# Score matmuls of differential attention on 128 rows, with stacked keys and head-wise projections

## The chip, the cores and the metric

The kernel runs on one core of a Trainium2 chip. The metric is the time of one execution on the device in microseconds (us). The engines are named as in the profile: PE is TensorE (matrix multiplications), PEld its weight loads, DVE is VectorE, ACT is ScalarE, POOL is GpSimd, SP is SyncE, which here only issues transfers. Each engine works through its own instruction list in order, and the engines wait for each other by semaphores. PSUM is the memory that PE writes, SBUF the one that it reads.

## The reference

A decoder trunk of two layers on 512 tokens of width 1024. Each layer normalizes x, projects it with one wide matrix, and runs three kinds of attention on parts of the result: differential attention (8 heads), latent attention (MLA, 8 heads) and attention into 256 memory tokens (cross, 4 heads). Their outputs are projected, gated, added and projected once more, and a squared-ReLU MLP follows. The change touches differential attention alone:

```python
def diff_attention(q, k, v, q_gain, k_gain, lam_vecs, out_gain, cos, sin, layer_idx):
    q = q.reshape(B, S, DIFF_HEADS, 2, DIFF_HEAD_DIM)      # 8 heads, 2 maps, 64
    k = k.reshape(B, S, DIFF_HEADS, 2, DIFF_HEAD_DIM)
    v = v.reshape(B, S, DIFF_HEADS, DIFF_V_DIM)            # 128
    q = rotary(rmsnorm(q, q_gain), c, s_)
    k = rotary(rmsnorm(k, k_gain), c, s_)
    o = causal_block_attention(q, k, v, DIFF_HEAD_DIM ** -0.5)
    ...
    o = o[:, :, :, 0, :] - lam.astype(o.dtype) * o[:, :, :, 1, :]
    o = rmsnorm(o, out_gain) * (1.0 - lam_init)
```

Each head has two score maps, each over 64 dimensions; the two softmaxes are subtracted with a factor and multiplied by one v.

## The kernel before

**Precision.** Operands of most matmuls are split into two parts, hi (rounded to the float32r type) and lo (the rest). A product is three matmuls: hi·hi, hi·lo, lo·hi. `mm3` (L108 to L111) issues the three for all projections. `split_into` (L100) makes the parts: ScalarE copies hi (L101), VectorE subtracts lo (L102).

**Weights.** Weights come from memory in units of at most 128x1024 (`wraw`, three buffers, L905) and are split into `whi` and `wlo` (four buffers each) ahead of use, in the order in which the program consumes them.

**Order.** `layer` builds a list of entries. Attention units are merged with GEMM entries stage by stage: `phases` (L882) names the attention units of nine stages, `PLAN` (L25) the GEMM groups that are spread between them by `merge` (L45). Stages 1 and 2 hold MLA, 3 holds cross attention, 4 to 7 hold two differential heads each (4 units a head), 8 none. In `PLAN`, `gx`, `gc` and `gd` are gate projections and what follows from them, `mem` the projections of memory tokens, `xq` the queries of cross attention, `ym` the output projection of MLA, and `d0` to `d3` the projections for differential attention. The framework then orders the instructions of each engine by a simulated timeline, with the program order as priority, so that work moves from its place in the list where a buffer or an operand is not there yet.

**Projections of differential attention.** `dpair(p)` (L858) makes three chunks for heads 2p and 2p+1: q, k and v, 256 columns each (`diff_chunk`, L553). A chunk is two entries of 96 matmuls in all; it fills two `psacc` buffers (there are two), each with two of the four token tiles, and `done` evicts each of these half chunks. For q and k: ScalarE copies it (L564) and squares it (L566), VectorE sums (L568), GpSimd takes the power −1/2 (L132), VectorE rotates and scales (L583 to L587), PE transposes (L591) into a `pstp` bank (there are two), and for each of the two heads `split_into` writes hi and lo of 128 rows, map 0 in rows 0 to 63 and map 1 in rows 64 to 127. V is copied with a scale (L561). All these results are tiles of the pool `B`, 24 of 128x512.

**Scores.** A unit of `diff_att` (L732) is one head and one block of 128 queries, with N = 128 to 512 keys. `scores` (L597) issues for each of the three hi/lo products the matmul of both maps in turn, into two of the three `pss` banks:

```python
            if diff:
                for i, (a, b) in enumerate(((0, 0), (0, 1), (1, 0))):
                    for m in range(2):
                        T.matmul(sw[m][:, :max(N, 256)], lhsT=qk[m][0][a], rhs=qk[m][1][b], start=i == 0, stop=i == 2)
```

This is L610: operands are slices of 64 rows. Then VectorE adds the mask (L622) and takes maxima (L624), ScalarE takes the exponential (L627), VectorE combines the maps (L630 to L632), PE transposes (L638) and multiplies with v (L642). There are 8 heads, 4 blocks and 2 layers: 64 units.

Of the kernel before, what the change touches and what calls it, by code (L numbers as in the profile page):

```python
# [24 lines left out]
PLAN = ["gx:1 K0 gx:1 Q0 gx:1 K1 gx:1 Q1", "gx mem", "xq d0", "d1 ym", "gc:6", "d2 gc", "d3", "gd:5", "gd"]  # L25
# [34 lines left out]
def tile_trunk(ctx: ExitStack, tc: tile.TileContext, x_t, mem_t, mem_n, pos, ifr, gcol, grow, w_ck, w_cq, w_kvb, w_qb,  # L60
# [68 lines left out]
    A.dma_start(out=gr, in_=grow[:, 0:128].partition_broadcast(P))  # L129

# [148 lines left out]
    def layer(l):  # L279
# [3 lines left out]
        def build_rope():  # L283
            for qk in range(2):
                a = sm.tile([P, NT, 64], F32, tag=f"ra{qk}", name=nm("ra"), bufs=1)
                b = sm.tile([P, NT, 64], F32, tag=f"rb{qk}", name=nm("rb"), bufs=1)
                for half in range(2):
                    g = gr[:, l, qk * 64 + half * 32:qk * 64 + (half + 1) * 32].unsqueeze(1).broadcast_to([P, NT, 32])
                    G.tensor_tensor(out=a[:, :, half * 32:(half + 1) * 32], in0=cosd, in1=g, op=ALU.mult)
                    G.tensor_tensor(out=b[:, :, (1 - half) * 32:(2 - half) * 32], in0=(sind if half == 0 else nsind), in1=g, op=ALU.mult)  # L290
                s["rope", qk] = (a, b)
# [261 lines left out]
        def diff_chunk(p, c):  # L553
            def done(tp, q):
                if tp == 0:
                    s["d", p, c] = [tl("B") for _ in range(2)] if c == 2 else [(tl("B", F32R), tl("B", F32R)) for _ in range(2)]
                dst = s["d", p, c]
                if c == 2:
                    for ti in range(2):
                        t = 2 * tp + ti  # L560
                        A.activation(out=dst[tp][:, ti * 256:(ti + 1) * 256], in_=q[:, ti * 256:(ti + 1) * 256], func=AF.Copy, scale=s["r"][:, t:t + 1])  # L561
                    return
# [8 lines left out]
                bc = lambda a: a[:, 2 * tp:2 * tp + 2].unsqueeze(2).broadcast_to([P, 2, 4])  # L571
                if c == 0:
                    V.tensor_tensor(out=ev, in0=sv, in1=bc(s["ex64"]), op=ALU.add)
                else:
                    V.scalar_tensor_tensor(out=ev, in0=sv, scalar=1.0 / 64, in1=bc(s["epsx"]), op0=ALU.mult, op1=ALU.add)
# [282 lines left out]
        def dpair(p):  # L858
            return diff_chunk(p, 0) + diff_chunk(p, 1) + diff_chunk(p, 2)
# [149 lines left out]
```

## Time and profile before

| what | value |
|---|---|
| median of 3 runs | 2037.0 us (2036.42 to 2038.12) |
| the profiled execution's own time | 2039.67 us |
| its span in the profile | 2037.6 us |
| PE busy | 2005.1 us (98%) |
| DVE busy | 1162.2 us (57%) |
| ACT busy | 917.4 us (45%) |
| POOL busy | 146.0 us (7%) |
| mean granted clock of PE | 0.994 |

The span reaches from the first to the last instruction of the program; the execution's own time is a little longer. Busy time of an engine is the time in which at least one of its instructions ran. Matmuls overlap in their pipeline, so the pace of PE is read from the starts of neighbouring instructions in the timeline and not from the duration of one. In the groups a line ends with its count, its busy time and the mean duration of one in ns, then the idle time of the engine before them. In the timeline a row gives start and length in us; neighbouring instructions of one kind are merged, with their count at the end.

### The profile page before, as it was taken

The page shows a single profiled execution, that of the slowest core. Times are in us where ns is not written, and L with a number is a line of the kernel's source. Part 1 is how long each engine was busy: PE and PEld are TensorE (multiplying, and loading weights), DVE is VectorE, ACT ScalarE, POOL GpSimd, SP SyncE. Part 2 cuts the span into 40 slices and gives each one's busy share as a digit, 9 for nine tenths or more (in the row PEclk, how much of TensorE's full clock was granted, in tenths as well). Part 3 has the DMA queues.
Part 4 walks back from the last instruction along what each step waited for, and adds up shares of the span by engine and source line. Part 5 has one row for each costly group of instructions (what it writes and reads, how often), then busy time and mean ns, then how long its engine had stood idle before and what let it go on. Part 6 is the DMA issues. An engine that isn't in the chain of part 4 may idle for free.

```text
span 2037.6 us, 27922 instructions
## 1 busy us (share of the span) xinstructions
PE 2005.1 (98%) x11008; PEld 1715.9 (84%) x11008; DVE 1162.2 (57%) x2170; ACT 917.4 (45%) x1727; POOL 146.0 (7%) x121
## 2 busy tenths in 40 slices
PE   8999999999999999999999999999999999999999
PEld 7779997888878888888888899979897788888887
DVE  7755765777656543434447567757686454434442
ACT  6666654444433432323346666634445334323321
POOL 0300110111200000000002001101020000000000
PEclk9989999999999999999999999999999999999999
DMA  5233122222214333333332321222222333333332
GB/s 170 73 110 102 69 63 73 63 73 73 63 53 154 93 96 101 93 99 98 117 104 67 125 80 63 72 74 63 73 63 63 101 116 93 102 96 94 102 94 73
DMA packets 54675, 181.06 MB, mean 89 GB/s; under 512 B 6416, under 2 KB 7440, under 8 KB 54544
## 3 DMA queue, kind: packets, MB, share of 16 engines
q1 hardware_dynamic: 51840, 175.66, 27.8%
q10 hardware_dynamic: 2704, 3.62, 0.6%
q8 instruction: 87, 1.43, 0.3%
q14 instruction: 44, 0.36, 0.1%
HBM read 175.06 MB, written 4.19 MB: 88 GB/s over the span
## 4 chain that ended last, share of the span: by engine, by line
PE 95%; ACT 2%; DVE 1%; DMA 1%; issue 0%; POOL 0%; ACTq 0%; DVEq 0%; POOLq 0%
PE psacc L109 21%; PE psacc L111 20%; PE psacc L110 20%; PE pss L109 7%; PE pss L111 7%; PE pss L110 7%; PE pss L610 2%; PE pss L613 2%; PE pso L642 2%; PE pstp L654 1%; PE pstp L638 1%; PE pstp L591 1%; PE pso L110 1%; PE pso L111 1%; PE pso L109 1%; PE pstp L479 1%
## 5 line engine op out<-in xcount | busy, mean ns | idle before, releaser
L101 ACT ACTIVATE whi<-wraw 128x1024 fp32r<-128x1024 f32 (+3 forms) x320 | 334.5, 1046 | 751.7 <-PE psacc L110 398.5
L102 DVE TENSOR_TENSOR wlo<-wraw,whi 128x1024 fp32r<-128x1024 f32 (+3 forms) x320 | 385.9, 1206 | 97.7 <-ACT whi L101 95.4
L109 PE MATMUL psacc<-H,whi 128*128 128x512 f32 x816 | 321.6, 394 | 2.6 <-ACT B L561 2.2
L110 PE MATMUL psacc<-H,whi 128*128 128x512 f32 x816 | 320.2, 392 | 0.0
L111 PE MATMUL psacc<-H,wlo 128*128 128x512 f32 x816 | 320.1, 392 | 0.0
L109 PE MATMUL psacc<-whi,H 128*128 128x256 f32 (+1 forms) x928 | 271.6, 294 | 10.3 <-ACT whi L101 6.8
L110 PE MATMUL psacc<-wlo,H 128*128 128x256 f32 (+1 forms) x928 | 265.1, 286 | 0.0
L111 PE MATMUL psacc<-whi,H 128*128 128x256 f32 (+1 forms) x928 | 264.3, 287 | 0.2 <-DVE H L106 0.2
L109 PE MATMUL pss<-O,whi 128*128 128x512 f32 x640 | 249.8, 392 | 1.6 <-ACT O L105 1.6
L110 PE MATMUL pss<-O,whi 128*128 128x512 f32 x640 | 250.8, 392 | 0.0
L111 PE MATMUL pss<-O,wlo 128*128 128x512 f32 x640 | 250.5, 392 | 0.0
L109 PEld LDWEIGHTS psacc<-whi,H 128*128 128x128 f32 x928 | 177.6, 192 | 17.8 <-ACT whi L101 6.8
L109 PEld LDWEIGHTS psacc<-H,whi 128*128 128x128 f32 x816 | 153.2, 188 | 36.0 <-ACT B L561 2.6
L111 PEld LDWEIGHTS psacc<-H,wlo 128*128 128x128 f32 x816 | 153.2, 188 | 33.6 <-issue 2.0
L110 PEld LDWEIGHTS psacc<-H,whi 128*128 128x128 f32 x816 | 153.3, 188 | 31.4 <-issue 0.7
L110 PEld LDWEIGHTS psacc<-wlo,H 128*128 128x128 f32 x928 | 178.2, 192 | 1.8 <-issue 1.0
L111 PEld LDWEIGHTS psacc<-whi,H 128*128 128x128 f32 x928 | 177.3, 192 | 1.0 <-DVE H L106 0.4
L840 DVE TENSOR_TENSOR X<-psacc,X 128x512 f32<-128x512 f32 x64 | 44.3, 692 | 207.1 <-PE psacc L111 207.1
L627 ACT ACTIVATE P<-pss,nmx 128x128 f32<-128x128 f32 (+2 forms) x224 | 115.1, 521 | 73.6 <-DVE nmx L624 47.5
L109 PEld LDWEIGHTS pss<-O,whi 128*128 128x128 f32 x640 | 120.4, 188 | 27.3 <-ACT O L105 2.0
L110 PEld LDWEIGHTS pss<-O,whi 128*128 128x128 f32 x640 | 121.1, 189 | 25.5 <-DVE O L106 0.3
L111 PEld LDWEIGHTS pss<-O,wlo 128*128 128x128 f32 x640 | 121.0, 189 | 24.9
(231 smaller groups left out, 3220.6 us busy)
## 6 DMA issues: line engine op xcount, KB each, us to landing
wraw<-in_w_dram SPq DMA_DIRECT2D x128, 512.0 KB, 3.6
wraw<-in_w_g_dram SPq DMA_DIRECT2D x48, 512.0 KB, 3.6
wraw<-in_w_d_dram SPq DMA_DIRECT2D x48, 512.0 KB, 3.6
wraw<-in_w_mem_dram SPq DMA_DIRECT2D x16, 512.0 KB, 3.7
wraw<-in_w_od_dram SPq DMA_DIRECT2D x16, 512.0 KB, 3.6
wraw<-in_w_out_dram SPq DMA_DIRECT2D x16, 512.0 KB, 3.7
X<-in_x_t_dram SPq DMA_DIRECT2D x16, 256.0 KB, 5.4
wraw<-in_w_xq_dram SPq DMA_DIRECT2D x8, 512.0 KB, 4.3
```

The source lines that it names most:

```text
L101: A.activation(out=hi, in_=src, func=AF.Copy)
L102: V.tensor_tensor(out=lo, in0=src, in1=hi, op=ALU.subtract)
L109: T.matmul(o, lhsT=l[0], rhs=r[0], start=first, stop=False, **kw)
L110: T.matmul(o, lhsT=l[0], rhs=r[1], start=False, stop=False, **kw)
L111: T.matmul(o, lhsT=l[1], rhs=r[0], start=False, stop=last, **kw)
L479: T.transpose(tp_[:96, t * P:(t + 1) * P], in_=src[t][:, h * 96:(h + 1) * 96], identity=ident)
L591: T.transpose(tp_[:, h * 256 + t * P:h * 256 + (t + 1) * P], in_=y[:, t * 256 + h * P:t * 256 + (h + 1) * P], identity=ident)
L610: T.matmul(sw[m][:, :max(N, 256)], lhsT=qk[m][0][a], rhs=qk[m][1][b], start=i == 0, stop=i == 2)
L613: T.matmul(sv[m], lhsT=qk[m][0], rhs=qk[m][1], start=True, stop=True)
L627: A.activation(out=pt[:, m, :N], in_=sv[m], func=AF.Exp, bias=nmx[:, m:m + 1], accum_out=ssum[m])
L642: T.matmul(o, lhsT=w[:, j * P:(j + 1) * P], rhs=vs(j), start=j == 0, stop=j == nb - 1)
L840: V.tensor_tensor(out=xt, in0=q, in1=xt, op=ALU.add)
```

## The change

- The q and k columns of the input projection are ordered by head: a chunk of 256 columns now holds q and k of one head (`head_chunk`), v keeps a chunk for two heads (`v_chunk`). The number of chunks and matmuls of the projections stays.
- `PLAN` names these chunks (`h0` to `h7`, `v0` to `v3`) in place of `d0` to `d3`, at other places between the attention units.
- For each map the keys' hi and lo lie in one tile `kk` of 128 rows, hi in the rows of the map and lo in the others. The queries' hi lies in both halves of `qh`, their lo in the rows of the map in `ql`, whose other half is set to zero by GpSimd. Two matmuls of 128 rows per map, `qh` with `kk` and `ql` with `kk`, give the sum of the three products.
- The eviction after the transposes is, for each of the two maps, three ScalarE copies and two VectorE subtractions of 64 rows and 256 columns.
- q and k share the formula for the norm, so the key gain is multiplied by 8 once at the start; the rope tables of q and k are two tiles in place of four, and the reversal of the halves moves from a multiplication to the addition.

```diff
-PLAN = ["gx:1 K0 gx:1 Q0 gx:1 K1 gx:1 Q1", "gx mem", "xq d0", "d1 ym", "gc:6", "d2 gc", "d3", "gd:5", "gd"]
+PLAN = ["gx:1 K0 gx:1 Q0 gx:1 K1 gx:1 Q1", "gx mem", "xq h0 v0", "h1 ym", "v1 h2 gc:5", "h3 v2 h4 gc:3", "h5 v3 h6 gc", "h7 gd:5", "gd"]
...
+    V.tensor_scalar(gr[:, :, 64:128], gr[:, :, 64:128], 8.0, None, ALU.mult)
...
+        def head_chunk(h):
+            def done(tp, q):
+                if tp == 0:
+                    qh, ql, kk = ([tl("B", F32R) for _ in range(2)] for _ in range(3))
+                    s["dh", h] = qh, ql, kk
+                    for m in range(2):
+                        G.memset(ql[m][(1 - m) * 64:(2 - m) * 64, :].bitcast(F32), 0.0)
+                qh, ql, kk = s["dh", h]
                 y = tl("scr")
                 A.activation(out=y, in_=q, func=AF.Copy)
                 z = tl("scr")
...
                 for ti in range(2):
-                    yv = y[:, ti * 256:(ti + 1) * 256].rearrange("p (g b d) -> p g b d", g=4, b=2)
-                    zv = z[:, ti * 256:(ti + 1) * 256].rearrange("p (g b d) -> p g b d", g=4, b=2)
-                    tab = lambda a: a[:, 2 * tp + ti, :].rearrange("p (b d) -> p b d", b=2).unsqueeze(1).broadcast_to([P, 4, 2, 32])
-                    V.tensor_tensor(out=zv, in0=yv[:, :, ::-1, :], in1=tab(b_), op=ALU.mult)
-                    V.tensor_tensor(out=yv, in0=yv, in1=tab(a_), op=ALU.mult)
-                V.tensor_tensor(out=y, in0=y, in1=z, op=ALU.add)
+                    v4 = lambda x: x[:, ti * 256:(ti + 1) * 256].rearrange("p (c g d) -> p c g d", c=2, g=2)
+                    tab = lambda x: x[:, 2 * tp + ti, :, :].unsqueeze(2).broadcast_to([P, 2, 2, 64])
+                    V.tensor_tensor(out=v4(z), in0=v4(y), in1=tab(b_), op=ALU.mult)
+                    V.tensor_tensor(out=v4(y), in0=v4(y), in1=tab(a_), op=ALU.mult)
+                rv = lambda x: x.rearrange("p (g b d) -> p g b d", g=8, b=2)
+                V.tensor_tensor(out=rv(y), in0=rv(y), in1=rv(z)[:, :, ::-1, :], op=ALU.add)
...
                 sl = slice(tp * 256, (tp + 1) * 256)
-                for h in range(2):
-                    split_into(dst[h][0][:, sl], dst[h][1][:, sl], tp_[:, h * 256:(h + 1) * 256])
-            return chunk256(w_d[l, c, p], x_h, 4, done)
+                for m in range(2):
+                    own, oth = slice(m * 64, (m + 1) * 64), slice((1 - m) * 64, (2 - m) * 64)
+                    qs, ks = tp_[own, 0:256], tp_[own, 256:512]
+                    copy_to(qh[m][own, sl], qs)
+                    copy_to(kk[m][own, sl], ks)
+                    copy_to(qh[m][oth, sl], qs)
+                    V.tensor_tensor(out=ql[m][own, sl], in0=qs, in1=qh[m][own, sl], op=ALU.subtract)
+                    V.tensor_tensor(out=kk[m][oth, sl], in0=ks, in1=kk[m][own, sl], op=ALU.subtract)
+            return chunk256(w_d[l, h], x_h, 4, done)
...
             if diff:
-                for i, (a, b) in enumerate(((0, 0), (0, 1), (1, 0))):
-                    for m in range(2):
-                        T.matmul(sw[m][:, :max(N, 256)], lhsT=qk[m][0][a], rhs=qk[m][1][b], start=i == 0, stop=i == 2)
+                for m in range(2):
+                    for i in range(2):
+                        T.matmul(sw[m][:, :max(N, 256)], lhsT=qk[m][0][i], rhs=qk[m][1], start=i == 0, stop=i == 1)
...
-                    qk = [([z[m * 64:(m + 1) * 64, qi * P:(qi + 1) * P] for z in q_[hh]], [z[m * 64:(m + 1) * 64, :W] for z in k_[hh]]) for m in range(2)]
+                    qk = [([z[m][:, qi * P:(qi + 1) * P] for z in (qh, ql)], kk[m][:, :W]) for m in range(2)]
```

More of the change, by code (lines that the diff above doesn't have):

```diff
@@ L551, in qb_item, with v_chunk @@
             return Entry(fn, [w_qb[l, hf][:, 0:2, :], w_qb[l, hf][:, 2:3, :]])
-        def diff_chunk(p, c):
+        def v_chunk(p):
             def done(tp, q):
                 if tp == 0:
[L556 to L562, printed above, removed]
+                    s["dv", p] = [tl("B") for _ in range(2)]
+                for ti in range(2):
+                    t = 2 * tp + ti
+                    A.activation(out=s["dv", p][tp][:, ti * 256:(ti + 1) * 256], in_=q[:, ti * 256:(ti + 1) * 256], func=AF.Copy, scale=s["r"][:, t:t + 1])
+            return chunk256(w_d[l, 8 + p], x_h, 4, done)
+        def head_chunk(h):
[6 more added lines that the diff above has]
+                qh, ql, kk = s["dh", h]
                 y = tl("scr")
@@ L856, in gy4 @@
             return r
-        def dpair(p):
-            return diff_chunk(p, 0) + diff_chunk(p, 1) + diff_chunk(p, 2)
         e = [Entry(lambda w: begin())]
@@ L865, in layer @@
         gd = [gate_item(0, ft, "B") for ft in range(KT)]
-        d0, d1, d2, d3 = (dpair(p) for p in range(4))
         cross = sum([cross_att(h) for h in range(4)], [])
@@ L872, in layer @@
         xq = xq_chunk(0) + xq_chunk(1)
-        groups = {"gx": gx, "K0": K0, "K1": K1, "Q0": Q0, "Q1": Q1, "mem": pre + mem, "xq": xq, "d0": d0, "d1": d1, "d2": d2, "d3": d3, "ym": ym, "gc": gc_, "gd": gd}
+        groups = {"gx": gx, "K0": K0, "K1": K1, "Q0": Q0, "Q1": Q1, "mem": pre + mem, "xq": xq, "ym": ym, "gc": gc_, "gd": gd}
+        groups.update({f"v{p}": v_chunk(p) for p in range(4)}, **{f"h{h}": head_chunk(h) for h in range(8)})
         def take(spec):
@@ L972, in _layout, with dcols @@
     d["w_xq"] = each(lambda l: blk(w_in[l][:, 3744:4256], 256))
-    d["w_d"] = each(lambda l: np.stack([blk(w_in[l][:, c * 1024:(c + 1) * 1024], 256) for c in range(3)]))
+    def dcols(l):
+        c = w_in[l][:, :3072].reshape(D, 3, 8, 128)
+        return np.concatenate([blk(c[:, 0:2, :, :].transpose(0, 2, 1, 3).reshape(D, 2048), 256), blk(c[:, 2].reshape(D, 1024), 256)])
+    d["w_d"] = each(dcols)
     d["w_g"] = each(lambda l: blk(w_in[l][:, 4256:7328], P))
```

26 lines of the change are left out of this document (12 added, 14 removed).

## The prediction

> **What bounds the kernel now.** I read the page first (busy shares and chain), then the stretches of layer 1 by stage, then the one group that the change rewrites, by shape and in the timeline.
>
> ```profile
> PE 2005.1 (98%) x11008; PEld 1715.9 (84%) x11008; DVE 1162.2 (57%) x2170; ACT 917.4 (45%) x1727; POOL 146.0 (7%) x121
> PE 95%; ACT 2%; DVE 1%; DMA 1%; issue 0%; POOL 0%; ACTq 0%; DVEq 0%; POOLq 0%
> ```
> ```profile
> 110.00:180.00 70.00, 63.42 (x380) 54.85 (x378) 40.41 (x77) 45.59 (x98) 2.71 (x3) 0.93 0.38 122
> 240.00:307.00 67.00, 67.00 (x520) 64.33 (x518) 47.97 (x99) 40.72 (x95) 11.30 (x6) 1.00 0.21 64
> 480.00:540.00 60.00, 57.63 (x412) 51.53 (x411) 47.01 (x115) 31.14 (x73) 16.47 (x13) 1.00 0.22 62
> ```
> The last three rows give a stretch, its length, and the busy time of PE, PE's weight loads, VectorE (DVE), ScalarE (ACT) and GpSimd (POOL), then granted clock and DMA. TensorE (PE) is the bound: 95% of the chain that ended last, and busy without a hole in the stretch from 240 to 307 us. Holes exist where attention has little GEMM work beside it (6.6 of 70 us from 110 to 180, 2.4 of 60 from 480 to 540). VectorE (47.0 of 60) and ScalarE (45.6 of 70) have room in every stretch. So an edit counts by the PE time it takes away, and by new PE waits that it makes. A busy PE is not PE at its pace, however: ends are modelled, so I price matmuls by start to next start.
>
> **The score matmuls.** Six matmuls of 64 rows per unit (two maps, three hi/lo products), 64 units: 384.
>
> ```profile
> L610 PE MATMUL pss<-B,B 64*128 64x256 f32 x192 | 28.6, 310 | 0.0
> L610 PE MATMUL pss<-B,B 64*128 64x512 f32 x96 | 21.5, 428 | 0.3 <-ACT P L627 0.3
> L610 PE MATMUL pss<-B,B 64*128 64x384 f32 x96 | 18.7, 370 | 0.0
> ```
> ```profile
> 539.58 0.96 PE L610 MATMUL pss<-B,B 64*128 64x512 f32 x3
> ```
> ```profile
> 566.96 0.97 PE L610 MATMUL pss<-B,B 64*128 64x512 f32 x6
> 567.86 0.50 PE L111 MATMUL psacc<-H,wlo 128*128 128x512 f32 x1
> 568.20 0.40 PE L109 MATMUL psacc<-H,whi 128*128 128x512 f32 x1
> ```
> Three matmuls of 512 columns stand 0.96 us, six stand 0.97 us: where both maps' matmuls follow each other, one in rows 0 to 63 and one in rows 64 to 127, the two run at the same time. So a third pass of both maps costs one slot, not two, and stacking to 128 rows gives that overlap up. Counting starts less than 20 ns apart over all 384 gives 110 pairs and 164 matmuls alone: 274 slots. They are alone where the scheduler had put one map's three matmuls apart from the other's. By columns (a mixed pair by its wider one) the slots are 136 of 256, 72 of 384 and 66 of 512.
>
> The price of a slot, in the pace of ordinary full-row matmuls:
>
> ```profile
> 61.93 0.39 PE L110 MATMUL psacc<-H,whi 128*128 128x512 f32 x1
> 62.16 0.39 PE L111 MATMUL psacc<-H,wlo 128*128 128x512 f32 x1
> 62.38 0.33 PE L109 MATMUL psacc<-whi,B 128*128 128x384 f32 x1
> 62.55 0.34 PE L110 MATMUL psacc<-wlo,B 128*128 128x384 f32 x1
> 62.73 0.34 PE L111 MATMUL psacc<-whi,B 128*128 128x384 f32 x1
> ```
> ```profile
> 403.52 0.28 PE L110 MATMUL psacc<-wlo,H 128*128 128x256 f32 x1
> 403.64 0.28 PE L111 MATMUL psacc<-whi,H 128*128 128x256 f32 x1
> 403.85 0.78 PE L610 MATMUL pss<-B,B 64*128 64x384 f32 x3
> 404.56 0.39 PE L109 MATMUL psacc<-whi,H 128*128 128x256 f32 x1
> 404.79 0.28 PE L110 MATMUL psacc<-wlo,H 128*128 128x256 f32 x1
> ```
> 512 columns 0.227 us, 384 columns 0.173, 256 columns 0.118 to 0.12. The 274 slots are 136 x 0.118 + 72 x 0.173 + 66 x 0.227 = 43.5 us.
>
> The same rows show something dearer: a toll on each change between full-row and half-row matmuls. Going in, 403.64 to 403.85 is 0.21 instead of 0.12 (+0.09). The three half-row matmuls of 384 take 0.71 instead of 3 x 0.173 = 0.52 (+0.19). And the first full-row matmul after them takes 404.56 to 404.79, 0.23 instead of 0.12 (+0.11); at 567.86 it is 0.34 instead of 0.227, again +0.11. Together 0.39 us for each run of score matmuls. The runs are 76; first and last:
>
> ```profile
> 307.14 0.62 PE L610 MATMUL pss<-B,B 64*128 64x256 f32 x3
> ...
> 1574.12 0.97 PE L610 MATMUL pss<-B,B 64*128 64x512 f32 x6
> ```
> 76 x 0.39 = 29.7 us. Summed run by run from the starts, waits taken out, the scores hold PE for 57.5 us, plus 7.9 going in and 7.9 in the first matmul after: 73.3 (the model gives 43.5 + 29.7 = 73.2).
>
> **What the change does to that.** Each map now has two matmuls of full rows: 64 units x 4 = 256, of them 128 of 256 columns (N is raised to 256 in the first block), 64 of 384, 64 of 512: 128 x 0.118 + 64 x 0.173 + 64 x 0.227 = 40.7 us, with no toll, since all neighbours are full-row too. Term: 40.7 - 73.3 = -32.6 us. Only 2.8 us of it come from fewer slots (274 to 256, a toll-free difference of 43.5 - 40.7); the rest is the toll. Weight loads fall by 128 as well; they lie beside matmuls now and count nothing, and stay beside them.
>
> Had all 384 run in pairs and without a toll, the old form would be 192 slots, 96 of 256 columns, 48 of 384 and 48 of 512: 30.5 us, and the change would add 10.2. The rows above say otherwise, and the sum goes by them. The TensorEngine Tiling (Array Packing) page of the Trainium skill, section Theoretical Speedup, gives up to 2x for a contraction of at most 64 rows, which speaks for the old form; the trace agrees for the 110 pairs and not for the 164 alone.
>
> **Evictions of q and k.** Before, a half chunk (two of the four token tiles) is evicted by two ScalarE copies and two VectorE subtractions of 128x256; now by six and four, of 64 rows and the same 256 columns.
>
> ```profile
> L101 ACT ACTIVATE B<-pstp 128x256 fp32r<-128x256 f32 x64 | 24.0, 382 | 43.6 <-PE pstp L591 33.1 <-DVE B L102 10.4
> L102 DVE TENSOR_TENSOR B<-pstp,B 128x256 fp32r<-128x256 f32 x64 | 26.5, 419 | 18.8 <-ACT B L101 11.9 <-PE pss L613 6.5
> L564 ACT ACTIVATE scr<-psacc 128x512 f32<-128x512 f32 x32 | 19.1, 596 | 14.1 <-PE psacc L111 13.9
> L566 ACT ACTIVATE scr<-scr 128x512 f32<-128x512 f32 x32 | 20.1, 630 | 0.5
> ```
> ```profile
> PE psacc L109 <- ACT scr L564: 2.2, 2, 1.1
> PE psacc L109 <- ACT B L561: 2.2, 2, 1.1
> ```
> Half the rows can cost from half to all of a full instruction; I take all of it, as the rows' times follow columns (0.382 for 256, 0.596 for 512). Per half chunk ScalarE gets 4 x 0.38 = 1.5 us more, VectorE 2 x 0.42 = 0.8 more; 32 half chunks, 49 and 27 us on engines that have 1120 and 875 us free. What can come through are PE waits at the head of a chunk, where a psacc buffer waits for ScalarE: 4.4 us in all today. If rebalancing removes them the term is -4.4. If they grow with the number of chunks in the differential stages (9 a layer for 6) and ScalarE's work per half chunk (3.5 us for 2.0), 4.4 becomes 11.7, so +7.3. I take +4, nearer that end, since ScalarE's queue is in order: a burst of six copies delays the weight splits and psacc copies queued behind it. VectorE's masks and maxima queue behind its four subtractions in the same way and are in this figure.
>
> **Small parts.** Rope tables: the same eight multiplications per layer, merged tiles; rotation: the same six VectorE operations per half chunk with the reversal in the addition; transposes: 4 per half chunk as before; q and k norms: one small operation each way; weights: the same 48 transfers, other columns. These cost nothing new. The padding adds 32 memsets of 64x512 on GpSimd, ahead of the power operation of the same chunk; GpSimd is busy for 7%. Four times the columns of its 128x128 memset bounds one at 0.2 to 0.8 us:
>
> ```profile
> masks.py:197 POOL MEMSET ident<- 128x128 f32 x1 | 0.2, 205 | 0.3 <-POOLq L997 0.3
> L132 POOL TENSOR_TENSOR f<-e,mhalf 128x8 f32<-128x8 f32 x32 | 66.6, 2080 | 183.9 <-DVE e L573 109.3 <-DVE e L575 74.6
> ```
> They can run while the chunk is still being multiplied, and the cover is a whole chunk (11.5 us); without it, two delay the 2.08 us power operation by at most 1.6 us, and the transposes behind it. Nothing on the path. B tiles: at most 24 are alive in the cross stage where 30 were wanted, so waits for them get rarer. I count no gain.
>
> The factor 8 on the key gains is a VectorE operation that waits for the small table gr:
>
> ```profile
> 2.14 0.46 ACTq L129 DMA_DIRECT2D gr<-in_grow_dram x1
> 4.56 0.17 DVE L142 CAST posf<-posi 128x4 f32<-128x4 int32 x1 [0.42 <-DMA posi<-in_pos_dram]
> 5.67 0.75 DVE L106 SCALAR_TENSOR_TENSOR H<-X,gc,H 128x512 fp32r<-128x512 f32 x1 [0.94 <-ACT H L105]
> 16.97 0.40 PE L111 MATMUL psacc<-whi,H 128*128 128x288 f32 x1 [0.20 <-DVE H L106]
> ```
> ```profile
> gr<-in_grow_dram ACTq DMA_DIRECT2D x1, 128.0 KB, 6.1
> ```
> gr lands at 2.1 + 6.1 = 8.2 us. If the scheduler puts the multiplication ahead of the first L106, VectorE's queue stands until then: 2.6 us later for the first low half, the weight splits behind it, and PE, which already waits for an L106 at 16.97. If it comes after 8.2 us it costs 0.1. I take +1.5.
>
> **Order of the GEMM work.** Stages 4 to 7 (differential attention) get more even filler. The MLA stage loses one chunk of 11.5 us and the cross stage two, 23 us; the cross stage had no hole at all, so I count nothing here and put its failure under the rivals.
>
> **Sum**: -32.6 + 4 + 1.5 = -27.1 us on the profiled execution, which took 2039.7 us (span 2037.6, 2.1 around it); that execution is 0.13% above the median of 2037.0, and I apply the difference to the median: 2010 us.
>
> **Rivals.** Thin filler (stays faster, by less): the MLA and cross stages, with 34 us less to hide latency, come to look like 110 to 180 us, with 6.6 us of hole each; at two stages and two layers 26 us at most, half of it 13: 2023. For it: ScalarE's 41 of 67 us in the cross stage must fit a shorter one. Against: the scheduler may pull later chunks forward.
>
> ScalarE burst (slower): place, the psacc copy behind the six copies; price, 1.5 us per half chunk when exposed, 49 in all. It decides from (32.6 - 1.5)/49, 63% exposed; at 80%, 39 us, 2037 - 31 + 39 = 2045. Against: today PE's waits for such copies are 4.4 us over the 48 half chunks of q, k and v.
>
> The overlap was worth more (slower): the pairs ran for nothing and the toll stays in another form, say between the transposes and the scores; then the passes count alone, 192 to 256 slots at best: +10.2, 2047. Against it are the 164 matmuls alone and the toll. It is the outcome by the 2x of the Trainium skill's page TensorEngine Tiling (Array Packing), section Theoretical Speedup.
>
> The change doesn't get the quick pass: the cross scores, also full-row and of 256 columns, have another pace.
>
> ```profile
> 305.50 0.81 PE L613 MATMUL pss<-B,B 128*128 128x256 f32 x3
> ```
> Three take 0.81 with 0.38 for the last one: 0.215 each, not 0.118. If writing the zeros as another type made the new operands run so, 40.7 becomes 74: +0.8 + 5.5, 2043. Against: the new tiles have the type of the old ones, whose 256 columns went at 0.118.
>
> **Chances.** Forecast 0.76 (its own range 2000 to 2018: all waits gone, -37; waits at +7.3 and gr at 2.6, -22.7, and a little beyond); thin filler 0.13; ScalarE burst 0.06; overlap 0.02; slow pass 0.03. What tells a change from none is about 0.2%, 4 us. Faster: all of the first, 0.10 of the second: 0.86. Same: 0.03 of the second, 0.02 of the burst near its break-even: 0.05. Slower: 0.04 + 0.02 + 0.03 = 0.09. The range reaches into thin filler, to 2026; 0.8 lies inside.
>
> **What would show it.** Score matmuls x256, 128*128, at 0.118, 0.173 and 0.227 start to start, with neighbours at their plain pace; PE busy about 28 us lower; waits of psacc for ScalarE under 12 us in all; no hole over 2 us a stage from 180 to 307. Wrong would be: a toll that stays around the scores, score matmuls at 0.215, or a VectorE stop before 8 us that PE passes on in full.

## The result, and the profile after

The changed kernel takes 2018.24 us (median of 4 runs, 2017.3 to 2019.04) against 2036.71 us for the kernel before (4 runs beside it, 2035.18 to 2038.12): −18.5 us, ratio 0.9909 with a 95% interval of 0.9892 to 0.9926. The profiled executions stand a little further apart: span 2017.2 us for 2037.6, −20.4 us (own times 2019.04 and 2039.67).

The page of the kernel after, its busy shares and then the shares of the chain that ended last:

```profile
PE 1976.3 (98%) x10880; PEld 1711.2 (85%) x10880; DVE 1187.2 (59%) x2235; ACT 961.9 (48%) x1855; POOL 155.7 (8%) x153
...
PE 91%; DVE 5%; ACT 2%; issue 1%; DMA 1%; POOL 0%; ACTq 0%; DVEq 0%; POOLq 0%
```

PE is busy for 28.8 us less (2005.1 before), as the prediction said. But the span fell by 8.4 us less than that, and VectorE's share of the chain went from 1% to 5%, which points to new waits for VectorE.

The score matmuls of the kernel after, grouped by shape, and one unit of four among its neighbours in the timeline:

```profile
L622 PE MATMUL pss<-B,B 128*128 128x256 f32 x128 | 25.3, 295 | 0.9 <-DVE B L606 0.6
L622 PE MATMUL pss<-B,B 128*128 128x512 f32 x64 | 18.7, 399 | 0.8 <-ACT P L639 0.8
L622 PE MATMUL pss<-B,B 128*128 128x384 f32 x64 | 14.7, 341 | 0.3
```
```profile
530.17 0.39 PE L111 MATMUL psacc<-H,wlo 128*128 128x512 f32 x1
530.40 1.07 PE L622 MATMUL pss<-B,B 128*128 128x512 f32 x4
531.31 0.39 PE L109 MATMUL psacc<-H,whi 128*128 128x512 f32 x1
531.53 0.39 PE L110 MATMUL psacc<-H,whi 128*128 128x512 f32 x1
```

There are 256, all of full rows. Going in takes 0.23 us, the four take 0.91 (4 x 0.227), the first matmul after them 0.22: the plain pace of 512 columns at all three places. The toll (the time that each run of half-row matmuls cost beyond its columns) is gone.

Now the stretches. Columns: stretch and length, then PE, PE's weight loads, VectorE, ScalarE, GpSimd (busy us and instructions), granted clock, DMA share, GB/s. First the kernel after in the MLA stage, the cross stage and the differential stages of layer 1, then the kernel before in the last of these:

```profile
110.00:180.00 70.00, 63.60 (x378) 54.81 (x377) 40.57 (x76) 46.12 (x98) 2.71 (x3) 0.93 0.40 125
240.00:307.00 67.00, 67.00 (x445) 61.38 (x443) 46.03 (x89) 44.82 (x112) 4.48 (x4) 1.00 0.19 57
300.00:560.00 260.00, 251.78 (x1673) 228.95 (x1672) 196.28 (x456) 145.51 (x328) 39.73 (x37) 1.00 0.23 70
```
```profile
300.00:560.00 260.00, 257.52 (x1597) 220.13 (x1596) 176.95 (x403) 124.41 (x284) 29.19 (x22) 1.00 0.23 69
```

The MLA stretch has its old holes (6.4 us, 6.6 before), and the cross stretch is still without one, although both lost filler. In the differential stages PE now stands idle for 8.2 of 260 us where it was 2.5. VectorE has 196 us of work there where it had 177. What PE waits for, over the whole run of the kernel after (us in total, times, longest):

```profile
PE psacc L109 <- DVE G L792: 3.4, 4, 1.1
PE psacc L109 <- DVE G L781: 3.2, 4, 1.1
PE psacc L109 <- ACT B L562: 2.9, 2, 1.4
PE pstp L597 <- DVE scr L593: 2.8, 4, 1.1
...
PE pss L622 <- DVE B L606: 0.6, 2, 0.3
PE psacc L109 <- ACT scr L574: 0.5, 2, 0.3
```

None of the VectorE rows shown here was there before. L781 and L792 are the evictions of gate chunks on VectorE, L593 is the scaling ahead of the transposes, L606 the last subtraction of a key part. Two rows of the kernel before have no counterpart; they lay at the end of the last head, ahead of the output projection:

```profile
PE pstp L669 <- DVE scr L666: 2.1, 2, 1.1
PE pss L109 <- ACT O L105: 1.6, 2, 0.8
```

**Where the time went, as a sum.** The rows of waits show only part of it, since a short delay is hidden in the modelled end of the matmul before. So I took the starts of all matmuls and subtracted, from each distance to the next start, the plain pace (0.118, 0.173 or 0.227 us by columns, 0.109 for a transpose). What is left over is the toll of half-row runs, time lost to waits, or time at a lower granted clock. In us:

| | before | after | difference |
|---|---|---|---|
| score matmuls at plain pace | 43.6 | 40.7 | −2.9 |
| toll, 0.39 for each of 76 runs, then 0 | 29.7 | 0 | −29.7 |
| over pace, ahead of the differential stages | 32.2 | 30.4 | −1.8 |
| over pace, differential stages | 10.6 | 31.7 | +21.1 |
| over pace, end of the last head | 7.4 | −0.1 | −7.5 |
| sum | | | −20.8 |

The sum is the difference of the spans (−20.4) within half a microsecond. That does not test the toll: the starts add up to the span whatever part of the rest is called toll. What bears on it are single rows, and all 76 runs of the kernel before: their medians over pace are 0.09 us going in, 0.20 inside and 0.11 in the first matmul after, 0.40 in all.

The granted clock has a part in the table too. Both traces hold stretches of 3.4 us, single or two on end, in which half the clock was granted while matmuls ran; each puts some 1.5 us over pace. The kernel before has seven of them (10.2 us), the kernel after four (6.0 us): 5.7 us for 4.5 ahead of the differential stages, 1.4 for 1.5 in them, and 3.1 for none at the end of the last head. There they are these two (the granted clock is the 0.50 behind the last pair of brackets; PE is busy throughout):

```profile
602.50:605.90 3.40, 3.40 (x9) 2.58 (x8) 1.83 (x4) 2.24 (x3) 0.00 (x0) 0.50 0.01 2
1609.40:1612.80 3.40, 3.40 (x9) 2.63 (x9) 1.64 (x3) 1.78 (x2) 0.00 (x0) 0.50 0.00 0
```

So some 4 of the 20.4 us are clock, and of the −7.5 us in the last line of the table only 4.4 are waits, the two rows above among them. The medians hold some of it as well. All runs of the kernel before were granted 0.994 to 0.997 of the clock, those of the kernel after 0.996 to 0.998; at 0.997 the kernel before took 2033.8 to 2036.3 us and the kernel after 2018.4, about 16 us less. Whether the change makes such stretches rarer was not tested.

The question is what makes the +21.1, and whether the toll is what I took it for.

### The profile page after: what moved, and what is told of

Same layout as the page of the kernel before. It is cut to its first block, busy times and chain, and to the rows that moved or that the text cites. A ratio compares the mean times of both kernels' runs of the same rounds, so it can differ in the third digit from the quotient of the medians.

```text
span 2017.2 us, 27896 instructions
## 1 busy us (share of the span) xinstructions
PE 1976.3 (98%) x10880; PEld 1711.2 (85%) x10880; DVE 1187.2 (59%) x2235; ACT 961.9 (48%) x1855; POOL 155.7 (8%) x153
## 4 chain that ended last, share of the span: by engine, by line
PE 91%; DVE 5%; ACT 2%; issue 1%; DMA 1%; POOL 0%; ACTq 0%; DVEq 0%; POOLq 0%
PE psacc L109 19%; PE psacc L110 19%; PE psacc L111 19%; PE pss L111 7%; PE pss L109 7%; PE pss L110 7%; PE pss L625 2%; PE pso L654 2%; PE pss L622 2%; PE pstp L666 1%; PE pstp L650 1%; DVE wlo L102 1%; PE pso L110 1%; PE pso L111 1%; PE pso L109 1%
## 5 line engine op out<-in xcount | busy, mean ns | idle before, releaser
L109 PEld LDWEIGHTS psacc<-H,whi 128*128 128x128 f32 x816 | 153.3, 188 | 35.7 <-DVE G L781 4.1
```

The lines of the kernel that those rows point to most:

```text
L109: T.matmul(o, lhsT=l[0], rhs=r[0], start=first, stop=False, **kw)
```

## The experiments

The expectations name the theories by letters. T: each run of half-row matmuls among full-row ones costs a toll of some 0.39 us, whatever it computes, and the gain of the change is that toll. P, against it: the gain lies in the number of passes, and half-row matmuls side by side are cheap. V: the new waits come from VectorE, whose queue got longer by four subtractions a half chunk. O: they come from the new order of the chunks in `PLAN`. H: they come from the turns that ScalarE's copies and VectorE's subtractions wait for each other. E: only what lies on the way of the eviction itself counts, not VectorE's work elsewhere. Each kernel was timed with runs of the kernel before on the same chip; differences below are between these medians, and the kernel after stands at −18.5 us by the same measure.

### Old scores in the new order

Head-wise chunks, `PLAN`, rotation and tables of the kernel after; evictions and scores of the kernel before.

```diff
-                    copy_to(qh[m][own, sl], qs)
...
-                    V.tensor_tensor(out=kk[m][oth, sl], in0=ks, in1=kk[m][own, sl], op=ALU.subtract)
+                split_into(q_[0][:, sl], q_[1][:, sl], tp_[:, 0:256])
+                split_into(k_[0][:, sl], k_[1][:, sl], tp_[:, 256:512])
...
-                for m in range(2):
-                    for i in range(2):
-                        T.matmul(sw[m][:, :max(N, 256)], lhsT=qk[m][0][i], rhs=qk[m][1], start=i == 0, stop=i == 1)
+                for i, (a, b) in enumerate(((0, 0), (0, 1), (1, 0))):
+                    for m in range(2):
+                        T.matmul(sw[m][:, :max(N, 256)], lhsT=qk[m][0][a], rhs=qk[m][1][b], start=i == 0, stop=i == 2)
```

> The head-wise chunks and the new order of the GEMM work, but the old evictions (two copies and two subtractions of 128x256 per half chunk) and the old scores (three products of 64 rows). The changed kernel took 2018 us: its scores cost 33 us less than before and its PE waits grew by 12 us. Theory V (the waits come from the two further VectorE subtractions per half chunk): the old load makes no new waits, so this run is within 4 us of before, 2033 to 2041. Theory O (the waits come from where the chunks and gates now lie): the waits stay, 2045 to 2051.

Measured: 2034.04 us (11 runs, 2031.44 to 2036.44) against 2036.26, −2.2 us; ratio 0.999 (0.9981 to 0.9999). Its differential stages in layer 1:

```profile
300.00:560.00 260.00, 256.78 (x1704) 224.25 (x1704) 179.18 (x422) 124.01 (x271) 34.15 (x27) 1.00 0.22 68
```

PE is idle for 3.2 us there, and the time over pace in all differential stages is 10.5 us less toll, about as before (10.6, with 1.4 of clock in it). The order makes no 21 us of new waits: O falls. It does take away the waits at the end of the last head (−0.2 us over pace for 7.4, of which 3.1 were clock): that part of the gain belongs to the new order and what came with it, not to the scores. It comes to little here because the scores fell into 84 runs instead of 76, with 101 pairs and 182 matmuls alone: +5.2 us of toll and slots. The −2.2 us itself is no more than clock: these runs were granted 0.997 to 1.000, and at 0.997 they took 2035.7 to 2036.4 us.

### Half rows for one of the two score matmuls

The operands of the kernel after; the product lo·hi is computed from the 64 rows that are not zero, so each unit has a full-row pair and a half-row pair.

```diff
-                for m in range(2):
-                    for i in range(2):
-                        T.matmul(sw[m][:, :max(N, 256)], lhsT=qk[m][0][i], rhs=qk[m][1], start=i == 0, stop=i == 1)
+                for i in range(2):
+                    for m in range(2):
+                        T.matmul(sw[m][:, :max(N, 256)], lhsT=qk[m][0][i], rhs=qk[m][1][i], start=i == 0, stop=i == 1)
...
-                    qk = [([z[m][:, qi * P:(qi + 1) * P] for z in (qh, ql)], kk[m][:, :W]) for m in range(2)]
+                    qk = [((qh[m][:, qi * P:(qi + 1) * P], ql[m][m * 64:(m + 1) * 64, qi * P:(qi + 1) * P]), (kk[m][:, :W], kk[m][m * 64:(m + 1) * 64, :W])) for m in range(2)]
```

> The changed kernel with the product of queries' lo and keys' hi as a matmul of 64 rows, the two maps' next to each other; the values are the same. Theory T (a toll of 0.39 us for each change between full-row and half-row matmuls, about 80 runs of scores): 2018 + 31, less up to 10 for the pairs that overlap, so 2037 to 2050. Theory P (only the number of passes counts, 192 slots where pairs overlap, 256 where not): 2008 to 2018.

Measured: 2052.76 us (2049.2 to 2054.75) against 2036.26, +16.5 us; ratio 1.0081 (1.0067 to 1.0095). That is 35 us more than the kernel after, for the same products and as many matmuls. A unit in its timeline (the four are two of full and two of half rows, one label for all):

```profile
312.30 0.28 PE L111 MATMUL psacc<-whi,H 128*128 128x256 f32 x1
312.41 0.71 PE L622 MATMUL pss<-B,B 128*128 128x256 f32 x4
313.05 0.39 PE L109 MATMUL psacc<-whi,H 128*128 128x256 f32 x1
313.27 0.28 PE L110 MATMUL psacc<-wlo,H 128*128 128x256 f32 x1
```

The first matmul after the half rows takes 0.22 us to the next start, again 0.10 above its pace. There are 105 runs of half-row matmuls. Read off the starts of all of them, the medians over pace are 0.10 us going in, 0.20 inside and 0.11 after: 0.40 us a run. By the difference of the times it comes out a little lower. Their slots are 16.5 us (23 pairs, 82 alone) where the full-row form has 20.4, so they saved 3.9 us and cost 35.0 + 3.9 in tolls: 0.37 us a run, if nothing else had changed. But these runs had less clock (0.992 to 0.997): the profiled one has five stretches at half of it in the differential stages (7.5 us over pace), the kernel after one. At 0.997 it took 2049.2 us, which leaves 0.33 us a run. The time lies some 3 us above what T expected. T stands, P falls. The Trainium skill, page TensorEngine Tiling (Array Packing), section Key Properties, says that a change of tiling mode drains TensorE; it gives no price. These runs agree with the rule, and give one: 0.33 to 0.40 us for a run of half-row matmuls, going in and coming out.

### Copies first, subtractions after

```diff
+                    copy_to(qh[m][oth, sl], tp_[own, 0:256])
+                for m in range(2):
+                    own, oth = slice(m * 64, (m + 1) * 64), slice((1 - m) * 64, (2 - m) * 64)
+                    V.tensor_tensor(out=ql[m][own, sl], in0=tp_[own, 0:256], in1=qh[m][own, sl], op=ALU.subtract)
...
```

> The changed kernel with all six ScalarE copies of a half chunk ahead of its four VectorE subtractions, in place of three, two, three, two. In the trace the second three copies waited for the subtractions of the first map. If these turns between the two queues are what holds the bank and the queues (theory H): 3 to 8 us faster than the changed kernel, 2010 to 2015. If VectorE's load alone counts (V), or the order of the chunks (O): within 2.5 us of 2018.

Measured: 2022.34 us (2021.33 to 2023.37) against 2036.26, −13.9 us; ratio 0.9934 (0.9921 to 0.9946). With both maps' copies ahead of the four subtractions the kernel is some 4.5 us slower than the kernel after, which neither theory had expected: H falls in this form.

### No subtractions

The lo parts of q and k are zero (set by GpSimd once a head), so only hi·hi counts in the scores; all matmuls and copies stay.

```diff
-                        G.memset(ql[m][(1 - m) * 64:(2 - m) * 64, :].bitcast(F32), 0.0)
+                        G.memset(ql[m].bitcast(F32), 0.0)
+                        G.memset(kk[m][(1 - m) * 64:(2 - m) * 64, :].bitcast(F32), 0.0)
...
-                    V.tensor_tensor(out=ql[m][own, sl], in0=qs, in1=qh[m][own, sl], op=ALU.subtract)
-                    V.tensor_tensor(out=kk[m][oth, sl], in0=ks, in1=kk[m][own, sl], op=ALU.subtract)
```

> The changed kernel without its four subtractions per half chunk; the lo parts of q and k are set to zero by GpSimd, so the scores are those of the hi parts alone. ScalarE's copies and all matmuls stay. Theory V: the waits of psacc and pstp for VectorE in the differential stages (about 10 us in all) fall below 4, and the time to 2008 to 2013. Theory O: they stay, 2016 to 2020.

Measured: 2007.75 us (2006.48 to 2009.39) against 2036.26, −28.5 us; ratio 0.9862 (0.9849 to 0.9876). That is 10 us less than the kernel after. The differential stages, and three rows of PE's waits:

```profile
300.00:560.00 260.00, 256.20 (x1693) 233.26 (x1692) 182.43 (x416) 146.63 (x333) 43.67 (x47) 1.00 0.23 72
```
```profile
PE psacc L109 <- ACT scr L575: 2.4, 6, 0.5
PE psacc L109 <- DVE G L791: 1.7, 4, 0.7
...
PE pstp L598 <- DVE scr L594: 0.7, 1, 0.7
```

PE's idle time in the stretch falls from 8.2 to 3.8 us; L791 and L594 (L792 and L593 in the kernel after) drop from 3.4 and 2.8 us to 1.7 and 0.7, and the row of the other gate eviction is gone. Over pace, the differential stages come to 20.0 us for 31.7, of which 1.5 are a stretch at half the clock that this trace does not have. So some 10 of the 21 us hang on the subtractions, as V has it. The zeros did not bring it by way of the clock: these runs were granted 0.997 to 0.998, those of the kernel after 0.996 to 0.998. Timeline of VectorE and PE around two waits of the kernel after:

```profile
384.78 0.42 DVE L605 TENSOR_TENSOR B<-pstp,B 64x256 fp32r<-64x256 f32 x1
385.21 0.42 DVE L606 TENSOR_TENSOR B<-pstp,B 64x256 fp32r<-64x256 f32 x1
385.65 0.69 DVE L591 TENSOR_TENSOR scr<-scr,scr 128x512 f32<-128x512 f32 x1
385.77 0.47 PE L622 MATMUL pss<-B,B 128*128 128x256 f32 x2 [0.30 <-DVE B L606]
...
386.49 0.68 DVE L593 TENSOR_TENSOR scr<-scr,f 128x512 f32<-128x512 f32 x1
...
387.31 0.63 PE L597 MATMUL pstp<-ident,scr 128*128 128x128 f32 x4 [1.07 <-DVE scr L593]
```

Two subtractions of 0.42 us stand ahead of the rotation's addition (L591) and the scaling (L593) of the next half chunk, without a gap between them; PE waits first for the subtraction, then 1.07 us for the scaling. The second wait is not made by the length of the subtractions, however: where they take 0.16 us each (narrow subtractions, below) it is 1.07 us as well. The groups of the evictions, by shape, in the kernel after:

```profile
L95 ACT ACTIVATE B<-pstp 64x256 fp32r<-64x256 f32 x192 | 65.7, 375 | 45.8 <-PE pstp L597 25.9 <-DVE B L606 18.5
L605 DVE TENSOR_TENSOR B<-pstp,B 64x256 fp32r<-64x256 f32 x64 | 26.8, 419 | 15.1 <-ACT B L95 13.8 <-PE pss L625 0.7
L606 DVE TENSOR_TENSOR B<-pstp,B 64x256 fp32r<-64x256 f32 x64 | 27.0, 422 | 0.9
```

Half the rows cost a full instruction (375 ns for 382, 419 and 422 for 419), as the prediction had taken it.

### The key gain's factor later

In the program, the multiplication moves behind the first work, into the preparation of the rope tables.

```diff
-    V.tensor_scalar(gr[:, :, 64:128], gr[:, :, 64:128], 8.0, None, ALU.mult)
...
+        V.tensor_scalar(gr[:, :, 64:128], gr[:, :, 64:128], 8.0, None, ALU.mult)
         posf = small("posf", NT, 1)
```

> The changed kernel with the factor 8 on the key gains applied after the first layer's row sums and no longer ahead of the first splits. In the trace of the changed kernel VectorE's first weight split stood behind it until 8.3 us (6.8 before) and PE stood 0.9 us more for it. If that delay reaches the end: 0.5 to 2 us faster than the changed kernel's 2018, so 2016 to 2017.5. If the first stage catches it up: 2018.

Measured: 2018.55 us (2016.85 to 2021.42) against 2037.64, −19.1 us; ratio 0.9909 (0.9896 to 0.9923): no difference from the kernel after. But the wait was not taken away. Timeline at the start of the kernel after, then of this one:

```profile
8.17 0.23 DVE L131 TENSOR_SCALAR gr<-gr 128x128 f32<-128x128 f32 x1 [1.61 <-DMA gr<-in_grow_dram]
8.31 0.75 DVE L102 TENSOR_TENSOR wlo<-wraw,whi 128x576 fp32r<-128x576 f32 x1
...
9.12 0.61 PE L110 MATMUL psacc<-wlo,H 128*128 128x288 f32 x1 [0.87 <-DVE wlo L102]
```
```profile
8.82 0.23 DVE L141 TENSOR_SCALAR gr<-gr 128x128 f32<-128x128 f32 x1 [2.18 <-DMA gr<-in_grow_dram]
9.77 0.61 PE L110 MATMUL psacc<-wlo,H 128*128 128x288 f32 x1 [1.44 <-DVE wlo L102]
```

In the kernel after, VectorE stands 1.61 us for the table and PE 0.87 us behind it. Here the framework again put the multiplication ahead of the first weight split, and PE stands 1.44 us: this run does not test what the wait costs. The starts tell it. The first 700 matmuls are the same in the kernels before and after. The first starts 0.13 us later after the change, the sixth 1.37 us (9.52 for 8.15), the 401st 0.52 us (88.02 for 87.50). So later waits in the start-up take up most of it, and some 0.4 us are left.

### Work moved from VectorE to GpSimd

Two kernels: the 64 sine products of the rotation (L588), and the 32 additions of gated outputs (L793).

```diff
-                    V.tensor_tensor(out=v4(z), in0=v4(y), in1=tab(b_), op=ALU.mult)
+                    G.tensor_tensor(out=v4(z), in0=v4(y), in1=tab(b_), op=ALU.mult)
```

> The changed kernel with the rotation's product by the sine table (two of VectorE's operations of 128x256 per half chunk, 0.8 us) on GpSimd, which is busy for 8%. Theory V (VectorE's queue sets the new waits): the same relief as one pair of subtractions, 3 to 6 us, 2012 to 2015, unless GpSimd's longer chain (2 x 0.9 us, ahead of or behind the power) shows up as waits of the transposes. Theory against it (what counts is the subtractions' place at the end of the chain, not VectorE's load): 2016 to 2022.

```diff
-                V.tensor_tensor(out=s["m", ft], in0=s["m", ft], in1=g, op=ALU.add)
+                G.tensor_tensor(out=s["m", ft], in0=s["m", ft], in1=g, op=ALU.add)
```

> The changed kernel with the addition of two gated outputs (VectorE, 128x512, 0.68 us, 16 per layer, in the differential stages and in the one after) on GpSimd. It stands in VectorE's queue between gates and chunks, but ends no chain that PE waits for soon. Theory V: 2 to 5 us faster than 2018. If only the eviction chain's own length counts: 2018 within 2 us.

Measured: 2020.49 us (2018.63 to 2020.97) and 2020.15 us (2019.24 to 2023.76) against 2037.64, −17.2 and −17.5 us; ratios 0.9914 (0.99 to 0.9927) and 0.9917 (0.9904 to 0.9931). Neither gains. For V the first one is not a clean test. Page and groups of the kernel with the products on GpSimd, then the same groups of the kernel after:

```profile
PE 1974.3 (98%) x10880; PEld 1709.6 (85%) x10880; DVE 1188.3 (59%) x2171; ACT 961.5 (48%) x1855; POOL 202.8 (10%) x217
```
```profile
L588 POOL TENSOR_TENSOR scr<-scr,rb 128x256 f32<-128x256 f32 x64 | 49.8, 799 | 242.3 <-DVE ss L578 212.2 <-DVE c L642 30.1
L589 DVE TENSOR_TENSOR scr<-scr,ra 128x256 f32<-128x256 f32 x64 | 31.1, 503 | 2.3 <-POOL scr L588 2.1
L678 DVE TENSOR_TENSOR scr<-scr,of 128x512 f32<-128x512 f32 x16 | 13.7, 859 | 5.4 <-POOL of L134 5.3
```
```profile
L589 DVE TENSOR_TENSOR scr<-scr,ra 128x256 f32<-128x256 f32 x64 | 24.6, 415 | 0.2
L678 DVE TENSOR_TENSOR scr<-scr,of 128x512 f32<-128x512 f32 x16 | 11.0, 685 | 4.6 <-POOL of L134 4.6
```

VectorE lost 64 instructions and is not less busy (1188.3 us for 1187.2): others became longer, L589 from 415 to 503 ns, L678 from 685 to 859. The Trainium skill, page SBUF — State Buffer, section Who interferes with whom, says that a VectorE instruction with two SBUF inputs and a GpSimd one that reads SBUF contend for a shared port pair. These means agree with it; that the pair is the cause was not tested apart.

### Less work on ScalarE: no third copy

The queries' hi isn't copied to the other half, which GpSimd sets to zero once a head; the product of hi(q) with lo(k) is left out.

```diff
+                        G.memset(qh[m][(1 - m) * 64:(2 - m) * 64, :].bitcast(F32), 0.0)
...
-                    copy_to(qh[m][oth, sl], qs)
```

> The changed kernel without the third ScalarE copy of each map (queries' hi in the other half); that half is zero, so the product of queries' hi and keys' lo is left out. ScalarE has 0.7 us less per half chunk, VectorE the same as in the changed kernel. The prediction's own reading (ScalarE's burst of copies makes the waits): 4 to 8 us faster than 2018. Theory V (VectorE makes them): within 2.5 us of 2018.

Measured: 2021.23 us (2017.42 to 2022.13) against 2037.64, −16.4 us; ratio 0.9916 (0.9902 to 0.9929). A third of the burst of six copies is gone and nothing is gained (35.7 us over pace in the differential stages for 31.7). PE's waits for `psacc` from ScalarE's evictions of q, k and v even grew, from 3.4 to 7.4 us. So nothing bears out the prediction's own reason for new waits, the burst on ScalarE. That a burst cut shorter still would give something is not excluded.

### Less work on VectorE elsewhere

The sine product of the rotation is left out (64 instructions ahead of L591), or the addition of the gated outputs (32 instructions that lie beside the chain of q and k).

```diff
-                    V.tensor_tensor(out=v4(z), in0=v4(y), in1=tab(b_), op=ALU.mult)
```

> The changed kernel without the rotation's product by the sine table (the addition after it adds the squares that stand in its operand): two VectorE operations of 128x256 fewer per half chunk, 0.83 us, and nothing put on GpSimd instead. It is the control for the run with that product on GpSimd, where VectorE's remaining operations became longer and its busy time hardly fell. Theory V (VectorE's load in the differential stages makes the waits, whatever operation it is): 2008 to 2013. Theory E (only the subtractions at the end of the eviction count): 2016 to 2021.

```diff
-                V.tensor_tensor(out=s["m", ft], in0=s["m", ft], in1=g, op=ALU.add)
```

> The changed kernel without the addition of two gated outputs, which no matmul waits for soon (8 per layer of 0.68 us in the differential stages, 8 after them). Theory V: a smaller relief of the same kind, 2 to 5 us, 2013 to 2016. Theory E: 2016 to 2021.

Measured: 2014.89 us (2012.06 to 2015.84) against 2036.94, −22.1 us, ratio 0.9885 (0.9871 to 0.9898) without the sine product; 2021.69 us (2020.69 to 2022.0), −15.3 us, ratio 0.9919 (0.9906 to 0.9933) without the addition. The differential stages without the addition:

```profile
300.00:560.00 260.00, 251.22 (x1673) 228.35 (x1672) 191.88 (x445) 143.66 (x327) 39.53 (x37) 1.00 0.23 70
```

VectorE has 4.4 us less work there than in the kernel after, and PE's idle time is 8.8 us for 8.2. So V falls in its general form, that any instruction less on VectorE is a wait less. Taking 27 us out of the rotation gave 3.6 us, less than V asked for and more than E did. Kernels from which work was only taken away came out 2 to 3 us slower (this one and the one without the third copy): each edit makes the framework order the instructions anew, so I read no single difference up to about 4 us as the effect of its edit. That holds for the 3.6 us too.

### lo of the queries once for both maps

A version that computes the same scores but for a product of two lo parts: one 128-row lo tile for q, its hi taken from an extra copy of 128 rows, one subtraction instead of two of 64 rows, no padding with zeros for q.

```diff
+                copy_to(qn, tp_[:, 0:256])
+                V.tensor_tensor(out=ql[:, sl], in0=tp_[:, 0:256], in1=qn, op=ALU.subtract)
...
-                    V.tensor_tensor(out=ql[m][own, sl], in0=qs, in1=qh[m][own, sl], op=ALU.subtract)
```

> A candidate: queries' lo of both maps in one tile of 128 rows, written by one VectorE subtraction of 128x256 from one further ScalarE copy; the zeros and their memsets go, and the other map's rows add a product of two lo parts, which is as small as what the split leaves out anyway. Per half chunk VectorE has 0.42 us less than the changed kernel, ScalarE 0.38 more. Theory V: half of the relief of leaving out all subtractions, less what ScalarE's seventh copy costs: 2012 to 2017. Theory E the same. If ScalarE's burst counts as much as VectorE's: 2018 to 2022.

Measured: 2028.98 us (5 runs, 2025.63 to 2031.01) against 2036.94, −8.0 us; ratio 0.9955 (0.9941 to 0.9968), 10.5 us slower than the kernel after and outside all that was expected. Its largest new row of PE's waits:

```profile
PE psacc L109 <- ACT scr L572: 12.2, 12, 1.4
```

One subtraction of four is saved a half chunk, but the copy of the next chunk out of `psacc` comes late. Three things changed for it: a seventh ScalarE instruction, one more `scr` tile out of a pool of five, and the order of the copies. Which of them it is was not separated.

### Narrow subtractions

All four subtractions stay, with their waits for ScalarE, but on 8 of their 256 columns; the rest of the lo parts is zero.

```diff
-                    V.tensor_tensor(out=ql[m][own, sl], in0=qs, in1=qh[m][own, sl], op=ALU.subtract)
+                    V.tensor_tensor(out=ql[m][own, n8], in0=tp_[own, 0:8], in1=qh[m][own, n8], op=ALU.subtract)
...
```

> The kernel without subtractions took 2008 us. This one has all four back per half chunk, at the same place and with the same waits between ScalarE and VectorE, but on 8 of 256 columns (the other lo parts are zero). If VectorE's time in the subtractions makes the waits (0.42 us each, here some 0.15): near that run, 2008 to 2012. If their turns with ScalarE's copies make them, whatever their length: near the changed kernel, 2015 to 2020.

Measured: 2009.94 us (2008.13 to 2010.7) against 2038.41, −28.5 us; ratio 0.9865 (0.9848 to 0.9881). Its group of the second subtraction, its differential stages, and two rows of PE's waits:

```profile
L608 DVE TENSOR_TENSOR B<-pstp,B 64x8 fp32r<-64x8 f32 x64 | 10.5, 164 | 0.9
```
```profile
300.00:560.00 260.00, 254.48 (x1688) 231.87 (x1687) 187.44 (x462) 146.62 (x335) 43.80 (x47) 1.00 0.24 73
```
```profile
PE pss L624 <- DVE B L608: 2.6, 2, 1.3
PE pstp L598 <- DVE scr L594: 2.1, 2, 1.1
```

Against the kernel before beside it, it gains as much as the kernel without subtractions, with as many subtractions as the kernel after; median against median it is 8.3 us faster than the kernel after. So their time of 0.42 us each is what counts (0.16 here), and not that they take turns with ScalarE: H falls again. Over pace, the differential stages come to 22.8 us. But the two rows, 2.6 and 2.1 us, were 0.6 and 2.8 in the kernel after, so it is not these waits that the short subtractions took away. The rows for the evictions of gate chunks did fall, from 3.4 and 3.2 us to one of 3.0. Which waits the 0.42 us lengthen, place by place, the runs don't settle.

## Why the prediction was right, and where it was off

**The toll: right.** The term was −32.6 us. After the change the slots cost 2.9 us less and the neighbours run at their plain pace, so the toll is gone. How large it was rests on the trace of before, 0.39 us read off rows and 0.40 as the median of all runs; the half-row kernel gives 0.40 by its starts and 0.33 to 0.37 by its time. PE's busy time fell by 28.8 us where some 28 were named.

**Evictions and new waits: the step that failed in its size, and in its reason.** The prediction took +4 us between −4.4 and +7.3, "since ScalarE's queue is in order: a burst of six copies delays the weight splits and psacc copies queued behind it". Measured is +21.1 us in the differential stages. The burst was not borne out as the cause: a third of it taken away gave nothing. Removing VectorE's subtractions, or making them short, gave 8 to 10 us. The prediction had named them too ("VectorE's masks and maxima queue behind its four subtractions") but gave them no price of their own. 27 us of new work on an engine that was busy for 57% cost some 8 to 10. The subtractions stand between the transposes and the scores, and ahead of the next half chunk's scaling; that PE loses the time just there is argued from their place and not shown, since rows of waits at both places stayed when the subtractions were short.

The bounds failed for a reason that can be read off. They were scaled from 4.4 us of rows of waits, while the starts show 10.6 us over pace in the same stages before the change, some 9 of them without the stretch at half the clock. The rows hold only what outlasts the modelled end of a matmul.

**What stays open.** Without the subtractions the differential stages still have 20.0 us over pace, with short ones 22.8, against 9 before (all without stretches at half the clock). 11 to 14 of the 21 us are thus not explained. The order of the chunks alone does not make them, nor does the third copy by itself, nor the additions on VectorE; the kernel without the sine product took 3.6 us off, no more than a reordering can do. No run leaves out both the subtractions and some copies, so ScalarE's part in this rest is open.

**The end of the last head: not in the prediction.** 4.4 us of waits went away there, and the kernel with the old scores in the new order does not have them either. Another 3.1 us were the two stretches at half the clock.

**Start and stages before.** The wait for the small table came one step later than the prediction had it, behind the first L106 and ahead of the first weight split. PE stood 0.87 us for it, and some 0.4 us of it are left where +1.5 was taken. Thin filler counted nothing, and that was right: no new hole from 110 to 307 us, and the time over pace ahead of the differential stages fell by 1.8 us, of which 1.2 are clock.

**The rivals.** Thin filler: its holes did not come. Its time of 2023 us is nearer to the measured one than the forecast's 2010, but only because the waits grew elsewhere. ScalarE burst: PE's waits for `psacc` from ScalarE's evictions of q, k and v are 3.4 us (L562 and L574), 4.4 before. Overlap worth more: the half-row kernel, whose matmuls could pair (23 pairs formed), is 35 us slower, not faster. Slow pass: 128 matmuls of 256 columns ran at 0.118 to 0.12 us like their neighbours.

**The sum.** −27.1 was forecast for the profiled execution, −20.6 came of its own times: 11.8 us more over pace, where waits were taken at 5.5. Without the clock the 11.8 would be 16, and here luck helped: 4.4 us of waits at the end of the last head and 4.2 us of clock, neither of them in the prediction, made up for part of the +21.1. On the medians it is −18.5, as the profiled run of the kernel before lay 3.0 us above its median and that of the kernel after 0.8. The measured 2018.2 us is at the edge of the forecast's own range (to 2018) and inside the range as a whole.

## What to carry to other kernels

Count the changes between half-row and full-row matmuls in PE's order, not only the passes: here a run of half-row matmuls cost some 0.4 us more than its columns. So 33% more passes by arithmetic (192 pairs to 256) came out as some 32.6 us less: 29.7 by the toll of 76 runs, and 2.9 because only 110 pairs had formed. Work added to an engine with room is not free: 27 us on VectorE at 57% cost 8 to 10 us, so give it a price of its own, where it stands in that engine's queue. Take waits from the starts of all matmuls against their plain pace: the rows of waits showed 4.4 us where some 9 were lost. And look at the granted clock of both profiles before a difference is read as waits: here it was 4 of 20 us. Last, see in the trace that an edit did what it was meant to do: the factor that was moved in the program ran at its old place.

## What the runs showed of the hardware that was not expected

- Evictions of 64 rows take as long as those of 128: 375 for 382 ns on ScalarE, 419 to 422 for 419 ns on VectorE, 256 columns each. The prediction had taken it as one of two bounds.
- In the profiles, half the clock was granted for stretches of 3.4 us while matmuls ran, most of them at places that changed from one kernel to the next (seven in the kernel before, four in the kernel after, two in the one without subtractions). Each cost some 1.5 us over pace.
- Work moved to GpSimd came back on VectorE: 64 products were 421 ns each there and 799 ns on GpSimd, and VectorE's busy time did not fall (1187.2 to 1188.3 us), as instructions beside them went from 415 to 503 and from 685 to 859 ns.
